# A two-layer hybrid mixer in fp32 on one core: TensorE in written order through the attention, two blocks turned ahead of their product, the next head's keys and values loaded one unit later

## The chip, the cores and the metric

The kernel runs on one core of one Trainium2 chip. The metric is the device time of one execution in microseconds (us). A run of the kernel before has a median of 3145.56 us.

## The reference

Two layers are computed for 1024 latent tokens and 256 context tokens, all in fp32, with a model width of 1024. In each layer one input projection feeds four token mixers: neighbourhood attention (`a`, 4 heads), multi-head latent attention (`m`, 4 heads), a recurrent scan (`lru`) and grouped-query attention (`g`, 4 heads). Their outputs are projected, weighted by sigmoid gates, summed, projected again and added to the stream. What matters here is the dense attention, which `g` and `m` share:

```python
def attend(q, keys, vals, scale):
    ...
    s = jnp.einsum('bkgqd,bknd->bkgqn', qg, keys, preferred_element_type=jnp.float32) * scale
    p = jax.nn.softmax(s, axis=-1).astype(vals.dtype)
    o = jnp.einsum('bkgqn,bknd->bkgqd', p, vals)
...
out = sum(jax.nn.sigmoid(ms[i]) * ((ys[i] * jax.nn.silu(zs[i])) @ w_branch[i]) for i in range(N_BRANCH)) @ w_out
```

Latent queries read all 1280 keys in `g` and `m`; in `a` they read a window of 8 by 16 latent tokens with a learned bias, and the context. Context queries read context only, and only in layer 0, because the second layer returns no context.

## The kernel before, in words

Every fp32 operand is held as a high and a low part, and a projection is three matmuls (high by high, low by high, high by low; `mm_b`, L284 to L286). ScalarE (ACT) casts the high part, VectorE (DVE) subtracts it from the source for the low part: `hi_lo` (L289 and L290) and, for weights, `split_w` (L238 and L239).

A layer runs through projections, the recurrent mixer woven between them, then the attention, then merge, and the output projection. In the attention twelve jobs, one for each head, follow each other: `g`, `m`, `a`, four heads each. A head goes through units of query tiles of 128 tokens: in layer 0 first a short unit of the two context tiles, in both layers then units of 3, 3 and 2 latent tiles. `attend` computes a unit:

- `scores` of one tile (L639): six matmuls for `g`, nine for `m`, into `wide`, three banks of PSUM of which there is one set. DVE moves it to `p` with its row minimum (L641), ACT takes the exponential (L615).
- `values` of a unit whose scores are done. It goes by blocks of 128 keys: `turn` transposes up to three tiles of `p` (L586) into one of two PSUM buffers `t`, ACT copies the high part to `ph` (L289), DVE subtracts for `pl` (L290); `product` adds the block into `pv` with two matmuls (L593 with `ph`, L594 with `pl`). The product of a block stands behind the turn of the next block. These steps are pumped between the scores of the following unit.
- `tick`, once per score tile and per block, adds now and then a group of six matmuls of the merge gates (`gates`, L284 to L286 into `g_att__mm`, `m_att__mm`, `a_att__mm`). Their weights come over ACT's DMA queue (L253), their results are copied by ACT (L938) and stored by a DMA that ACT issues (L939).

The queries of a unit come by DMAs on the queue of SyncE (SP) into one of three buffers `q` (L651, for `m` also L653 for the rotary part), one unit ahead. The keys `ks` (L660), values `vs` (L665) and for `a` two bias tables (`be`, `bm`) of the next head come on the same SP queue: `ahead_kv` is called at the first unit of a head.

The program is written in this order, but a list scheduler of the framework sets the order of every engine's queue, by priorities and a model of durations, unless an engine is pinned with `manual_schedule`. Tiles come from pools: `sl` holds 13 slots of 5 KB per partition (keys, values, probabilities, `y`, the scan's buffers), `wp` holds 10 pairs of high and low weights.

Of the kernel before, what the change touches and what calls it, by code (L numbers as in the profile page):

```python
# [17 lines left out]
KC = D // 128  # L18
# [21 lines left out]
UNITS = [(2, 3), (5, 3), (8, 2)]  # L40
NBIAS = (E_N + M_N) * 64
# [5 lines left out]
def hybrid_kernel(ctx: ExitStack, tc, a):  # L47
# [5 lines left out]
    wp = ctx.enter_context(tc.tile_pool(name="wp", bufs=10))  # L53
    sl = ctx.enter_context(tc.tile_pool(name="sl", bufs=13))
    tp = ctx.enter_context(tc.tile_pool(name="tp", bufs=2))
    sm = ctx.enter_context(tc.tile_pool(name="sm", bufs=6))
# [60 lines left out]
    def spare():  # L117

        turns[0] += 1
        tag = ("tmp", "ph", "tmp", "pl", "tmp", "ph", "pl")[turns[0] % 7]  # L120
        return tp.tile([128, 512], F32, tag=tag, name=nm("spare"), bufs=3 if tag == "tmp" else 2)
# [72 lines left out]
    def row_stats(src):  # L194
        st = sm.tile([128, 2, 6], F32, tag="bnst", name=nm("bnst"))
# [36 lines left out]
    def split_w(raw, shape):  # L232
        n = 1
        for d in shape[1:]:
            n *= d
        hi = wp.tile([128, 512], F32R, tag="whi", name=nm("whi"))
        lo = wp.tile([128, 512], F32R, tag="wlo", name=nm("wlo"))
# [7 lines left out]
    def load_w(src, shape):  # L245
# [8 lines left out]
        return split_w(raw, shape)  # L254

    def load_rows(w2, c0, n):
        return [load_w(w2[k * 128:(k + 1) * 128, c0:c0 + n], [128, n]) for k in range(KC)]
# [34 lines left out]
    def layer(l, xh, xl, need_ctx, gate, finish, side, side2, ahead=None):  # L292
# [27 lines left out]
        def put_t(dst, t, first, src, rows=128):  # L320
# [6 lines left out]
            hi = tp.tile([128, 4, 128], F32R, tag="ph", name=nm("th"), bufs=2)  # L327
# [8 lines left out]
        def put_v(dst, t, src3):  # L336

            n = src3.shape[1]
            vt = tp.tile([128, 4, 128], F32R, tag="ph", name=nm("vt"), bufs=2)
# [226 lines left out]
        def attend(h, unit, qs, y, rcp, scores, vt):  # L566
# [7 lines left out]
            queue.append([values(64 * (h % 2), y, qts, blocks, pts, vt), len(blocks) + 1])  # L574

        def values(o, y, qts, blocks, pts, vt):
# [5 lines left out]
            def turn(vb, q0, cols):  # L582
# [4 lines left out]
                ph = tp.tile([128, 512], F32R, tag="ph", name=nm("ph"), bufs=2)  # L587
# [8 lines left out]
            st = None  # L596
            for i, b in enumerate(blocks):
                nx = turn(*b)
                tick()
                if st:  # L600
                    product(i - 1, *st)
                st = nx
                yield
            product(nb - 1, *st)
# [111 lines left out]
        def m_steps():  # L716
            gm, mrope_c, mrope_s, wraws, wu = pre[0]
            wm = [split_w(r, [128, 416]) for r in wraws]
# [23 lines left out]
            def second(t, has_q, y, kr):  # L742
# [4 lines left out]
                ch = tp.tile([128, 512], F32R, tag="ph", name=nm("ch"), bufs=2)  # L747
# [138 lines left out]
        def attention(jobs):  # L886
# [22 lines left out]
            for n, (job, i) in enumerate(steps):  # L909
                label, h, branch, units, _, begin, _ = job  # L910
                fetch(n + 1)
                if i == 0:
                    j = jobs.index(job) + 1
                    if j < len(jobs):
                        ahead_kv(j)
                    head = begin(kv[label, h])
# [38 lines left out]
        for _ in att:  # L955
            pass
        flush()
# [58 lines left out]
        for c in range(KC):  # L1016
# [14 lines left out]
            wo[0].append(load_w(a["w_out"][l, c * 128:(c + 1) * 128, :512], [128, 512]))  # L1031
# [201 lines left out]
```

## Time and profile before

| | |
|---|---|
| three runs | 3131.25, 3145.56 (median), 3148.48 us |
| profiled execution: time / span | 3149.83 / 3148.0 us |
| granted TensorE clock, mean | 0.949 |
| attention of layer 0 | from 403 to 1163 us |
| attention of layer 1 | from 2085 to 2738 us |
| DMA, mean | 95 GB/s |

The profile is of one execution. Busy time of TensorE (PE) is the sum of stretches in which a matmul is shown at work. The clock of 1.00 is 2.4 GHz; where the rows show less, TensorE ran at 1.2 GHz in part of the stretch.

### The profile page before, as it was taken

The numbers are of one execution on the slowest core, as the hardware profiler recorded it, in microseconds if no ns is written. First come the engines' busy times: TensorE is split into PE (matmuls) and PEld (weight loads), VectorE is DVE, ScalarE is ACT, GpSimd is POOL, SyncE is SP. The second block draws the span as 40 slices with busy tenths as digits, with TensorE's granted clock in tenths as the row PEclk, the third lists the DMA queues.
The fourth block names the chain that finished last, engine by engine and source line by source line (L and its number), as shares of the span: only waits on it lengthen the run. The fifth ranks groups of instructions, "written<-read, shape, count | busy, mean of one in ns | idle before, by whom it ended". The sixth has DMA issues, their size and how long they took to land.

```text
span 3148.0 us, 39813 instructions
## 1 busy us (share of the span) xinstructions
PE 2837.8 (90%) x14458; PEld 2292.2 (73%) x14458; DVE 1554.1 (49%) x3147; ACT 1270.7 (40%) x2698; POOL 235.2 (7%) x327
## 2 busy tenths in 40 slices
PE   7987979998988999999789897998999897999878
PEld 3766868787877787776457685877887786788657
DVE  5653365554545551222368644366654464523366
ACT  4353364544444451111233435265544454512230
POOL 1210000000000000000342110000000000000141
PEclk9998989998999999999799999998999998999999
DMA  7232422222323222322462323322332233212252
GB/s 256 86 106 88 118 66 65 83 89 67 92 85 97 92 94 65 71 60 90 157 173 78 119 75 115 112 83 72 89 94 75 84 102 96 78 47 64 89 159 77
DMA packets 308782, 299.83 MB, mean 95 GB/s; under 512 B 24553, under 2 KB 245993, under 8 KB 308585
## 3 DMA queue, kind: packets, MB, share of 16 engines
q1 hardware_dynamic: 177384, 202.49, 21.3%
q10 hardware_dynamic: 131200, 94.79, 9.8%
q8 instruction: 114, 1.87, 0.3%
q14 instruction: 84, 0.68, 0.1%
HBM read 217.11 MB, written 80.10 MB: 94 GB/s over the span
## 4 chain that ended last, share of the span: by engine, by line
PE 65%; DMA 15%; DVE 7%; ACT 4%; POOL 3%; issue 3%; SPq 2%; ACTq 1%; POOLq 0%; DVEq 0%
PE wide L639 5%; PE merge__mm L284 4%; PE merge__mm L285 4%; PE merge__mm L286 4%; PE wide L284 2%; PE wide L285 2%; PE wide L286 2%; PE m_att__t L586 2%; PE a_att__mm L284 2%; PE a_att__mm L285 2%; PE a_att__mm L286 2%; DMA g_att__q<-start__qkg 2%; PE g_att__t L586 2%; PE m_att__mm L286 2%; PE m_att__mm L284 2%
## 5 line engine op out<-in xcount | busy, mean ns | idle before, releaser
L284 PE MATMUL merge__mm<-xh,merge__whi 128*128 128x512 f32 (+1 forms) x640 | 240.5, 376 | 1.2 <-DVE a_att__tmp L439 1.2
L285 PE MATMUL merge__mm<-xl,merge__whi 128*128 128x512 f32 (+1 forms) x640 | 236.7, 370 | 0.0
L286 PE MATMUL merge__mm<-xh,merge__wlo 128*128 128x512 f32 (+1 forms) x640 | 236.6, 370 | 0.0
L290 DVE TENSOR_TENSOR m_att__pl<-m_att__t,m_att__ph 128x384 fp32r<-128x384 f32 (+1 forms) x248 | 121.5, 507 | 141.3 <-ACT m_att__ph L289 138.2
L289 ACT CAST m_att__ph<-m_att__t 128x384 fp32r<-128x384 f32 (+1 forms) x248 | 105.7, 441 | 148.1 <-PE m_att__t L586 101.0
L238 ACT CAST merge__whi<-merge__wraw 128x512 fp32r<-128x512 f32 (+1 forms) x112 | 59.3, 530 | 236.0 <-PE merge__mm L285 179.3
L284 PEld LDWEIGHTS merge__mm<-xh,merge__whi 128*128 128x128 f32 x640 | 121.1, 189 | 41.5 <-issue 16.5
L239 DVE TENSOR_TENSOR merge__wlo<-merge__wraw,merge__whi 128x512 fp32r<-128x512 f32 (+1 forms) x112 | 64.5, 576 | 166.2 <-ACT merge__whi L238 158.4
L290 DVE TENSOR_TENSOR g_att__pl<-g_att__t,g_att__ph 128x384 fp32r<-128x384 f32 (+1 forms) x228 | 112.8, 514 | 68.0 <-ACT g_att__ph L289 64.6
L999 DVE TENSOR_TENSOR merge__tmp<-wide,merge__tmp 128x512 f32<-128x512 f32 (+1 forms) x80 | 50.9, 637 | 176.2 <-PE wide L286 168.3
L639 PE MATMUL wide<-g_att__ks,g_att__q 128*128 128x512 f32 (+1 forms) x400 | 112.4, 380 | 26.6 <-DMA g_att__q<-start__qkg 14.0
L286 PEld LDWEIGHTS merge__mm<-xh,merge__wlo 128*128 128x128 f32 x640 | 121.3, 189 | 20.7
L289 ACT CAST g_att__ph<-g_att__t 128x384 fp32r<-128x384 f32 (+1 forms) x228 | 99.6, 446 | 89.5 <-PE g_att__t L586 80.4
L285 PEld LDWEIGHTS merge__mm<-xl,merge__whi 128*128 128x128 f32 x640 | 121.2, 189 | 19.1
L284 PE MATMUL wide<-merge__uh,merge__whi 128*128 128x512 f32 (+1 forms) x240 | 100.5, 419 | 36.9 <-DVE merge__tmp L999 26.4
L284 PE MATMUL a_att__mm<-xh,a_att__whi 128*128 128x512 f32 (+1 forms) x320 | 126.2, 395 | 0.3 <-DVE a_att__tmp L439 0.3
L993 ACT ACTIVATE merge__tmp<-merge__mm 128x512 f32<-128x512 f32 (+1 forms) x80 | 44.2, 553 | 199.6 <-PE merge__mm L286 198.4
L593 PE MATMUL m_att__pv<-m_att__ph,m_att__vs 128*128 128x384 f32 (+1 forms) x228 | 88.8, 389 | 37.3 <-ACT m_att__ph L289 37.2
L285 PE MATMUL a_att__mm<-xl,a_att__whi 128*128 128x512 f32 (+1 forms) x320 | 121.9, 381 | 0.0
L641 DVE TENSOR_SCALAR_CACHE_REDUCE m_att__p<-wide 128x1280 f32<-128x1280 f32 (+1 forms) x72 | 98.7, 1371 | 46.1 <-PE wide L639 43.1
L286 PE MATMUL a_att__mm<-xh,a_att__wlo 128*128 128x512 f32 (+1 forms) x320 | 121.1, 380 | 0.0
L639 PE MATMUL wide<-m_att__ks,m_att__q 128*128 128x512 f32 (+1 forms) x400 | 120.8, 372 | 0.4 <-DVE m_att__p L641 0.4
(415 smaller groups left out, 8060.7 us busy)
## 6 DMA issues: line engine op xcount, KB each, us to landing
merge__wraw<-in_w_in_dram SPq DMA_DIRECT2D x64, 256.0 KB
mod__wm<-in_w_mod_dram SPq DMA_DIRECT2D x48, 256.0 KB
g_proj__wm<-in_w_mod_dram SPq DMA_DIRECT2D x16, 512.0 KB
a_att__wraw<-in_w_in_dram ACTq DMA_DIRECT2D x32, 256.0 KB
last__wraw<-in_w_out_dram SPq DMA_DIRECT2D x32, 256.0 KB
g_att__wraw<-in_w_in_dram ACTq DMA_DIRECT2D x28, 256.0 KB
m_att__wraw<-in_w_in_dram ACTq DMA_DIRECT2D x28, 256.0 KB
merge__wraw<-in_w_branch_dram SPq DMA_DIRECT2D x48, 128.0 KB
```

Source lines behind the costliest of these rows:

```text
L238: act.copy(hi[:, :n], raw[:, :n])
L239: dve.tensor_sub(lo[:, :n], raw[:, :n], hi[:, :n])
L284: pe.matmul(ps, wh, xh, start=first and k == 0, stop=False)
L285: pe.matmul(ps, wh, xl, start=False, stop=False)
L286: pe.matmul(ps, wl, xh, start=False, stop=last and k == nk - 1)
L289: act.copy(hi, src)
L290: dve.tensor_sub(lo, src, hi)
L586: pe.transpose(tb[:, i * 128:(i + 1) * 128], pts[q0 + i][:, col:col + 128], ident)
L593: pe.matmul(pv[:, qr], vt[:, vb, :], ph, start=i == 0, stop=False)
L639: pe.matmul(wide[:, c0:c0 + w], qs[:, j, qi * 128:(qi + 1) * 128], k[:, c0:c0 + w], start=j == 0, stop=j == len(ks) - 1)
L641: dve.tensor_scalar(pt[:, :nk], wide[:, :nk], -scale, None, ALU.mult, ALU.min, accum_out=nb)
L999: dve.tensor_mul(sgm[:, :g[1]], pb[:, :g[1]], sgm[:, :g[1]])
```

## The change

TensorE's queue keeps the order in which the program is written, from the first score of the attention to its last product. A block's product stands behind the turns of the two blocks that follow it (`AHEAD`), and the last products of a unit are steps of their own. The next head's keys and values are requested at a head's second unit. The slots become 16 and the weight pairs 6; to make room for eight weights at a time, half of the weights of a projection's eight row blocks (`far`) lie as a pair in one slot. A third `ph` buffer is added; some small tiles and a scratch area shrink. Line numbers move by 6 to 10.

```diff
+AHEAD = 2
-    wp = ctx.enter_context(tc.tile_pool(name="wp", bufs=10))
-    sl = ctx.enter_context(tc.tile_pool(name="sl", bufs=13))
+    wp = ctx.enter_context(tc.tile_pool(name="wp", bufs=6))
+    sl = ctx.enter_context(tc.tile_pool(name="sl", bufs=16))
-    sm = ctx.enter_context(tc.tile_pool(name="sm", bufs=6))
+    sm = ctx.enter_context(tc.tile_pool(name="sm", bufs=4))
...
-    def split_w(raw, shape):
+    def split_w(raw, shape, far=False):
...
+        if far:
+            both = slot(F32R, w=1024, s="wboth")
+            hi, lo = both[:, :512], both[:, 512:]
+        else:
+            hi = wp.tile([128, 512], F32R, tag="whi", name=nm("whi"))
+            lo = wp.tile([128, 512], F32R, tag="wlo", name=nm("wlo"))
...
-        return [load_w(w2[k * 128:(k + 1) * 128, c0:c0 + n], [128, n]) for k in range(KC)]
+        return [load_w(w2[k * 128:(k + 1) * 128, c0:c0 + n], [128, n], k >= 4) for k in range(KC)]
...
-            queue.append([values(64 * (h % 2), y, qts, blocks, pts, vt), len(blocks) + 1])
+            queue.append([values(64 * (h % 2), y, qts, blocks, pts, vt), len(blocks) + AHEAD])
...
-                ph = tp.tile([128, 512], F32R, tag="ph", name=nm("ph"), bufs=2)
+                ph = tp.tile([128, 512], F32R, tag="ph", name=nm("ph"), bufs=3)
...
-            st = None
+            turned = []
             for i, b in enumerate(blocks):
-                nx = turn(*b)
+                turned.append(turn(*b))
                 tick()
-                if st:
-                    product(i - 1, *st)
-                st = nx
+                if len(turned) > AHEAD:
+                    product(i - AHEAD, *turned.pop(0))
                 yield
-            product(nb - 1, *st)
+            for j, st in enumerate(turned):
+                product(nb - len(turned) + j, *st)
+                if j < len(turned) - 1:
+                    yield
...
                 if i == 0:
+                    head = begin(kv[label, h])
+                if i == 1:
                     j = jobs.index(job) + 1
                     if j < len(jobs):
                         ahead_kv(j)
-                    head = begin(kv[label, h])
...
-        for _ in att:
-            pass
-        flush()
+        with tc.manual_schedule(engines={mybir.EngineType.PE}):
+            for _ in att:
+                pass
+            flush()
...
-            wo[0].append(load_w(a["w_out"][l, c * 128:(c + 1) * 128, :512], [128, 512]))
+            wo[0].append(load_w(a["w_out"][l, c * 128:(c + 1) * 128, :512], [128, 512], 2 <= c < 6))
```

The first place is the SP queue in layer 0, inside the second `m` head, at the load of the third one's keys and values. Before:

```order
L653 DMA m_att__q_6511<-start__qkm_107 64x1x384
L651 DMA m_att__q_6674<-start__qkm_107 128x1x384
L660 DMA m_att__ks_6516<-start__qkm_107 128x1x1280
L665 DMA m_att__vs_6518<-start__vm_110 128x10x128
L653 DMA m_att__q_6674<-start__qkm_107 64x1x384
L651 DMA m_att__q_6674<-start__qkm_107 128x1x384
L653 DMA m_att__q_6674<-start__qkm_107 64x1x384
L651 DMA m_att__q_6755<-start__qkm_107 128x1x256
```

And now:

```order
L661 DMA m_att__q_6656<-start__qkm_107 64x1x384
L659 DMA m_att__q_6741<-start__qkm_107 128x1x256
L668 DMA m_att__ks_6661<-start__qkm_107 128x1x1280
L673 DMA m_att__vs_6663<-start__vm_110 128x10x128
L661 DMA m_att__q_6741<-start__qkm_107 64x1x256
L659 DMA m_att__q_6741<-start__qkm_107 128x1x256
L661 DMA m_att__q_6741<-start__qkm_107 64x1x256
L659 DMA m_att__q_6924<-start__qkm_107 128x1x256
```

The load stood among the queries of the head's third unit (three tiles, 384 columns) and stands among those of its fourth (two tiles, 256 columns).

The second place is TensorE's queue in the same head, behind its short unit: the end of the scores of one tile, what stands between, and the next tile's. Before:

```order
L639 MATMUL wide<-m_att__krs_5208,m_att__q_6511 128x256
L284 MATMUL m_att__mm_6627<-xh,m_att__whi_6623 128x256
L285 MATMUL m_att__mm_6627<-xl,m_att__whi_6623 128x256
L286 MATMUL m_att__mm_6627<-xh,m_att__wlo_6624 128x256
L284 MATMUL m_att__mm_6627<-xh,m_att__whi_6623 128x256
L285 MATMUL m_att__mm_6627<-xl,m_att__whi_6623 128x256
L286 MATMUL m_att__mm_6627<-xh,m_att__wlo_6624 128x256
L586 MATMUL m_att__t_6712<-ident,m_att__p_6520 128x128
L586 MATMUL m_att__t_6712<-ident,m_att__p_6583 128x128
L586 MATMUL m_att__t_6719<-ident,m_att__p_6520 128x128
L586 MATMUL m_att__t_6719<-ident,m_att__p_6583 128x128
```

And now:

```order
L647 MATMUL wide<-m_att__krs_5352,m_att__q_6497 128x256
L592 MATMUL m_att__t_6705<-ident,m_att__p_6502 128x128
L592 MATMUL m_att__t_6705<-ident,m_att__p_6563 128x128
L599 MATMUL m_att__pv_6678<-m_att__ph_6682,m_att__vs_6054 128x256
L600 MATMUL m_att__pv_6678<-m_att__pl_6683,m_att__vs_6054 128x256
L647 MATMUL wide<-m_att__ks_6052,m_att__q_6497 128x512 x2
L647 MATMUL wide<-m_att__krs_5352,m_att__q_6497 128x512
```

Ten matmuls and four more of the gates stood between the scores of the head's first two latent tiles; between those of the second and the third there are now four.

The third place is a block in the middle of a unit of the same head. Before, and then now:

```order
L586 MATMUL m_att__t_6828<-ident,m_att__p_6679 128x128
L586 MATMUL m_att__t_6828<-ident,m_att__p_6692 128x128
L586 MATMUL m_att__t_6828<-ident,m_att__p_6728 128x128
L593 MATMUL m_att__pv_6773<-m_att__ph_6803,m_att__vs_5796 128x384
L594 MATMUL m_att__pv_6773<-m_att__pl_6804,m_att__vs_5796 128x384
L586 MATMUL m_att__t_6838<-ident,m_att__p_6679 128x128
```

```order
L592 MATMUL m_att__t_6812<-ident,m_att__p_6665 128x128
L592 MATMUL m_att__t_6812<-ident,m_att__p_6692 128x128
L592 MATMUL m_att__t_6812<-ident,m_att__p_6714 128x128
L599 MATMUL m_att__pv_6759<-m_att__ph_6779,m_att__vs_6054 128x384
L600 MATMUL m_att__pv_6759<-m_att__pl_6780,m_att__vs_6054 128x384
L592 MATMUL m_att__t_6822<-ident,m_att__p_6665 128x128
```

The pair `ph_6803`, `pl_6804` belongs to the block turned before the one shown; `ph_6779`, `pl_6780` belongs to the one two blocks before.

## Rows read from the trace of the kernel before

**Rows 1.** The page, part 1 (busy time) and part 4 (the chain that ended last).

```profile
PE 2837.8 (90%) x14458; PEld 2292.2 (73%) x14458; DVE 1554.1 (49%) x3147; ACT 1270.7 (40%) x2698; POOL 235.2 (7%) x327
...
PE 65%; DMA 15%; DVE 7%; ACT 4%; POOL 3%; issue 3%; SPq 2%; ACTq 1%; POOLq 0%; DVEq 0%
```

**Rows 2.** TensorE by stretch, layer 0: length, busy (instructions), clock, DMA share, GB/s.

```profile
403.00:444.00 41.00, 22.69 (x91) 0.71 0.16 45
...
488.00:504.00 16.00, 12.04 (x60) 0.89 0.18 60
...
504.00:604.00 100.00, 99.70 (x596) 1.00 0.27 79
...
604.00:630.00 26.00, 20.03 (x100) 0.87 0.16 55
...
730.00:764.00 34.00, 23.54 (x121) 0.75 0.21 66
...
864.00:904.00 40.00, 29.91 (x164) 0.83 0.33 100
...
1004.00:1024.00 20.00, 11.48 (x55) 0.74 0.27 91
...
1064.00:1084.00 20.00, 14.92 (x67) 0.83 0.34 104
```

**Rows 3.** The same view in layer 1.

```profile
2106.00:2166.00 60.00, 47.14 (x248) 0.86 0.34 94
...
2386.00:2426.00 40.00, 35.00 (x182) 0.91 0.29 85
...
2426.00:2466.00 40.00, 36.03 (x185) 0.96 0.24 73
...
2466.00:2506.00 40.00, 34.15 (x178) 0.91 0.33 100
...
2600.00:2620.00 20.00, 15.86 (x77) 0.83 0.38 113
...
2646.00:2686.00 40.00, 28.30 (x138) 0.83 0.29 89
```

**Rows 4.** The timeline of SP's queue: start, duration, line, operation.

```profile
719.54 2.19 SPq L665 DMA_DIRECT2D m_att__vs<-start__vm  x1
721.77 15.28 SPq L653 DMA_DIRECT2D m_att__q<-start__qkm  x1
```

**Rows 5.** The timeline of ACT: start, duration, operation, idle before and releaser.

```profile
744.63 0.33 ACTq L939 DMA_DIRECT2D start__gates<-m_att__tmp  x1
745.28 0.37 ACT L289 CAST m_att__ph<-m_att__t 128x256 fp32r<-128x256 f32 x1 [10.09 <-DMA m_att__q<-start__qkm]
```

**Rows 6.** The timeline of TensorE, at the start of the attention and later.

```profile
417.12 0.39 PE L284 MATMUL g_att__mm<-xh,g_att__whi 128*128 128x512 f32 x1
...
417.34 0.39 PE L285 MATMUL g_att__mm<-xl,g_att__whi 128*128 128x512 f32 x1
...
438.12 2.50 PE L639 MATMUL wide<-g_att__ks,g_att__q 128*128 128x512 f32 x6 [8.59 <-DVE g_att__p L641]
...
745.71 0.58 PE L593 MATMUL m_att__pv<-m_att__ph,m_att__vs 128*128 128x256 f32 x1 [9.16 <-ACT m_att__ph L289]
```

**Rows 7.** The timeline of DVE at the start of layer 0's attention.

```profile
435.09 0.17 DVE L458 TENSOR_SCALAR lru__sp<-lru__lrucols 128x4 f32<-128x4 f32 x1 [12.88 <-DMA lru__lrucols<-in_lru_cols_dram]
```

**Rows 8.** The chain of waits, layer 1's start: start, duration.

```profile
2135.85 12.49 DMA g_att__wraw<-in_w_in_dram
```

**Rows 9.** Groups of instructions, both attentions: count, busy, mean ns, idle before and releasers.

```profile
L641 DVE TENSOR_SCALAR_CACHE_REDUCE m_att__p<-wide 128x1280 f32<-128x1280 f32 (+1 forms) x72 | 98.7, 1371 | 46.1 <-PE wide L639 43.1 <-PE m_att__t L586 2.1
...
L615 ACT ACTIVATE m_att__p<-m_att__p,m_att__nb 128x1280 f32<-128x1280 f32 (+1 forms) x72 | 91.6, 1272 | 42.1 <-DVE m_att__p L641 41.5
...
L289 ACT CAST m_att__ph<-m_att__t 128x384 fp32r<-128x384 f32 (+1 forms) x248 | 105.7, 441 | 148.1 <-PE m_att__t L586 101.0 <-DMA m_att__q<-start__qkm 26.4 <-DMA a_att__ks<-outp__qka 8.0
...
L290 DVE TENSOR_TENSOR m_att__pl<-m_att__t,m_att__ph 128x384 fp32r<-128x384 f32 (+1 forms) x248 | 121.5, 507 | 141.3 <-ACT m_att__ph L289 138.2
```

More of the change, by code (lines that the diff above doesn't have):

```diff
@@ L120, in spare @@
         tag = ("tmp", "ph", "tmp", "pl", "tmp", "ph", "pl")[turns[0] % 7]
-        return tp.tile([128, 512], F32, tag=tag, name=nm("spare"), bufs=3 if tag == "tmp" else 2)
+        return tp.tile([128, 512], F32, tag=tag, name=nm("spare"), bufs=2 if tag == "pl" else 3)
     def bank():
@@ L194, in row_stats @@
     def row_stats(src):
-        st = sm.tile([128, 2, 6], F32, tag="bnst", name=nm("bnst"))
+        st = sm.tile([128, 2, 6], F32, tag="bnst", name=nm("bnst"), bufs=2)
         for i in range(2):
@@ L235, in split_w @@
             n *= d
-        hi = wp.tile([128, 512], F32R, tag="whi", name=nm("whi"))
-        lo = wp.tile([128, 512], F32R, tag="wlo", name=nm("wlo"))
+        if far:
[4 more added lines that the diff above has]
+            lo = wp.tile([128, 512], F32R, tag="wlo", name=nm("wlo"))
         act.copy(hi[:, :n], raw[:, :n])
@@ L243, in split_w, with load_w @@
         return hi[:, :n], lo[:, :n]
-    def load_w(src, shape):
+    def load_w(src, shape, far=False):
         n = 1
@@ L253, in load_w @@
         wq[0].dma_start(dst, src)
-        return split_w(raw, shape)
+        return split_w(raw, shape, far)
     def load_rows(w2, c0, n):
-        return [load_w(w2[k * 128:(k + 1) * 128, c0:c0 + n], [128, n]) for k in range(KC)]
+        return [load_w(w2[k * 128:(k + 1) * 128, c0:c0 + n], [128, n], k >= 4) for k in range(KC)]
     def load_rows2(w2, c0):
@@ L326, in put_t @@
                 pe.transpose(pt[:r, i * 128:(i + 1) * 128], s, ident)
-            hi = tp.tile([128, 4, 128], F32R, tag="ph", name=nm("th"), bufs=2)
+            hi = tp.tile([128, 4, 128], F32R, tag="ph", name=nm("th"), bufs=3)
             lo = tp.tile([128, 4, 128], F32R, tag="pl", name=nm("tl"), bufs=2)
@@ L338, in put_v @@
             n = src3.shape[1]
-            vt = tp.tile([128, 4, 128], F32R, tag="ph", name=nm("vt"), bufs=2)
+            vt = tp.tile([128, 4, 128], F32R, tag="ph", name=nm("vt"), bufs=3)
             hi_lo(vt[:, :n, :64], vt[:, :n, 64:], src3)
@@ L717, in m_steps @@
             gm, mrope_c, mrope_s, wraws, wu = pre[0]
-            wm = [split_w(r, [128, 416]) for r in wraws]
+            wm = [split_w(r, [128, 416], k >= 4) for k, r in enumerate(wraws)]
             def first(t, ps):
@@ L746, in second @@
                     pe.transpose(pt[:, b * 128:(b + 1) * 128], y[:, b * 128:(b + 1) * 128], ident)
-                ch = tp.tile([128, 512], F32R, tag="ph", name=nm("ch"), bufs=2)
+                ch = tp.tile([128, 512], F32R, tag="ph", name=nm("ch"), bufs=3)
                 cl = tp.tile([128, 512], F32R, tag="pl", name=nm("cl"), bufs=2)
@@ L1221 @@
     }
-    nc = bacc.Bacc("TRN2", target_bir_lowering=False, num_devices=1, dynamic_dma_scratch_size=1024)
+    nc = bacc.Bacc("TRN2", target_bir_lowering=False, num_devices=1, dynamic_dma_scratch_size=64)
     arrays, args = {}, {}
```

## The prediction

> **What bounds the kernel now.** First the page: TensorE (PE) is busy 90% of the span and holds 65% of the chain that ended last; DMAs hold 15% of that chain, more than any other engine [rows 1]. So PE's work is the floor, and what can be won is PE standing still, or running at half its clock after it stood. Next the stretches of PE in the two attentions, which are the only stages whose order the change pins [rows 2, 3]. A clean stretch, as that from 504 to 604, is busy 99.70 of 100 us at a clock of 1.00. The losses sit in islands. I cost an island as its idle time plus (1 − clock) times its busy time, which is about what the clock takes away.
>
> - Layer 0 [rows 2]: the start, 403 to 444, loses 18.3 + 6.6 = 24.9 us. The six islands after it lose 5.3, 8.6, 16.3, 15.2, 11.5 and 7.6, together 64.5.
> - Layer 1 [rows 3]: the start, 2106 to 2166, loses 12.9 + 6.6 = 19.5 us. The five islands after it lose 8.2, 5.4, 8.9, 6.8 and 16.5, together 45.8.
>
> That is 155 us in all, and the most that better order can win here.
>
> Last, who makes an island. I follow the one at 730 to 764. PE waits 9.16 us at 745.71 for `ph`, ACT's copy [rows 6]. ACT waited 10.09 us, not for PE but for a DMA of `q`; in front of the copy it had issued a store of a gate [rows 5]. SP's queue shows why that `q` is late: the values `vs` of the next head go out at 719.54, and the next DMA, a piece of `q`, holds the queue for 15.28 us, to 737.05 [rows 4]. The load of keys and values stands in front of queries that are wanted soon, and ACT, which issues DMAs in between its copies, is held with them. Over both attentions ACT's `ph` in the `m` heads waits 26.4 us for such a `q` [rows 9]. The DMA engines themselves are busy only 0.13 to 0.34 of the time in these islands (0.16 to 0.38 with layer 1's) [rows 2, 3]: it is a queue that is full, not a bandwidth.
>
> **The change, part by part.**
>
> *The load one unit later, layer 0.* From 719.54 to the moment PE stopped (745.71 − 9.16 = 736.55) is 17 us of cover; ACT was released at 745.28 less its copy's hand-over, some 26 us after the load [rows 4 to 6]. Before, the cover was one short context unit and one unit of three tiles. Now it is two units of three tiles. Layer 0's attention takes 760 us for 144 score tiles (12 heads of 2 context and 10 latent tiles), 5.3 us each, so six tiles are an estimated 32 us. 32 is more than 26: where this pattern stands alone, the island goes. Two things keep part of it. ACT's DMAs stand earlier in line than PE's scores, so ACT meets the backlog before the 32 us are over; and for `a` heads the two bias tables follow in the same place. I keep 18 of the 64.5 us (three islands of the smaller size, 5.3 to 8.6): a gain of 46.5. The bounds are 0, if the backlog only meets other work, and 64.5.
>
> *The same in layer 1.* There is no context unit there: the cover was six latent tiles and is now five, the load stands before the next head's first queries and not before a head's last. PE's own need is no better covered; what changes is which of ACT's DMAs stand behind it. Between 0 and 45.8 I take two fifths, a gain of 18, because the islands here [rows 3] are the same kind at ACT but nothing in the order removes their cause.
>
> *Layer 1's start.* The chain shows a gate weight that lands 12.49 us after its issue [rows 8]; with 10 weight pairs five chunks of gate weights (two pairs each) could be ahead, now three can, and casts come later in ACT's queue. Between 0 and 19.5 I take a gain of 11.5.
>
> *Layer 0's start.* DVE stands 12.88 us for `lrucols` of the next layer's scan, hoisted in front of the scores [rows 7], and PE then waits 8.59 us at its scores [rows 6]. In the new order that instruction still stands there, ahead even of the second score. In the order before, 48 gate matmuls stood ahead of the first score and filled the scan's tail; matmuls of 512 columns start 0.22 us apart there (417.12, 417.34) [rows 6], so that filling was worth up to 11 us. Pinned, no gate matmul may pass the first score. I charge 8 us; bounds 0 and 11, plus a second wait of 8.59 if the scores stand twice.
>
> *Written order behind a short unit.* Scores use the one `wide`, and the next tile's wait for DVE's 1.371 us [rows 9]. Where 14 matmuls stood between two tiles there are now four, two transposes and two products, and behind the next unit's first scores its transposes need the last tile's exponential (1.371 + 1.272 us [rows 9]) sooner. By 0.22 us for a 512-column matmul, four smaller ones cover at most 0.5 us: 0.9 us are open at the first place, some 0.3 at the second. 12 heads by 1.2 us is 14 us, in layer 0 only. Bounds: 0 and 12 × 2.6 = 32.
>
> *Written order elsewhere.* Some 208 latent tiles (72 `g`, 72 `m`, 64 `a`, less what layer 0's short units already paid). A block turned needs ACT 0.441 and DVE 0.507 us [rows 9] before its product. One block behind, a transposition and a product stand between, about as much; two blocks behind, twice that, so that an exponential of 1.272 us in front of a copy is partly covered. The clean stretches carry the same load and idle 0.3% [rows 2]. I charge 5 us; bounds 0 and 62 (0.3 us for each tile).
>
> *Edits that I cost at nothing.* Slots, weight pairs, small tiles and the scratch: the counts of casts, subtractions and DMAs stay. In the projections and the woven scan `far` weights hold four slots, three of which are new. What hides a later weight is PE's backlog of other products; without that cover a slot that comes late costs one scan step. I bound it by −5 and +15 us.
>
> **The sum.** −46.5 − 18 − 11.5 + 8 + 14 + 5 = −49. The profiled execution took 3149.8 us, which makes 3100.8; it lies 4.3 above the median of the runs, 3145.56, so the forecast is **3097 us**.
>
> **The rivals.**
>
> *A. Nearly all of it goes.* If both layers' islands and layer 1's start go, and written order costs nothing: −64.5 − 45.8 − 19.5 = −130, that is 3016 us; with half of the costs charged, about 3030. For it: all islands have the queue in common. Against: layer 1's cover does not grow.
>
> *B. The backlog only moves.* The same bytes go through the same SP queue, and the piece behind them still waits 15 us [rows 4]; other queries and other stores of ACT are held instead. Then 3149.8 − 11.5 + 8 + 14 + 5 = 3165, less 4.3 = 3161 with the costs, 3134 without them. Against: of two loads of one kind only those with a short cover show an island, and 504 to 604 runs clean [rows 2]. The Trainium skill (Perfetto Trace Analysis, What "DMA-bound" means) holds that an issuing engine whose track is solid with DMA slices is bound by descriptor generation, and that larger descriptors are the cure; by that this move wins nothing. The trace agrees that the track is solid behind a load [rows 4], not that it is so between loads.
>
> *C. Slower: PE stands at every tile.* Before, the scheduler put gate matmuls where PE would wait; pinned, PE meets each score, transposition and product in program order, and a late DVE or ACT stops all that is behind it. Place: the wait of the next scores for `wide` and of transposes for PSUM's two `t`. Price: at 0.6 us for each of 208 tiles 125 us, against the other gains and losses of −46.5 − 18 − 11.5 + 8 = −68: 3149.8 + 57 − 4 = 3203 us. It decides from 68 / 208 = 0.33 us for each tile. For it: the first place above shows such a wait. Against: blocks are turned two ahead, and the gate matmuls still come every few steps. The Trainium skill (TensorE: Matmul & The Clock Gate, A second HAM failure mode: psum-queue depth-cycling) tells of a kernel whose frequent short pauses between groups of matmuls dropped the clock again and again; by the islands' ratio in layer 0 (45% on top of the idle time) that would make 3259. The trace so far speaks against it: from 2426 to 2466 PE idles 10% and the granted clock is 0.96 [rows 3].
>
> That the change does nothing, because the scheduler kept written order anyway, is ruled out by the rows of the order.
>
> **How the numbers follow.** A measurement of this kernel can tell a difference of about 0.5% (16 us) from none: below 3130 is faster, above 3161 slower. My forecast, 3065 to 3125: 0.50. Better than that, towards A: 0.13. B and half-way to it, 3125 to 3165: 0.20, of which 0.04 faster, 0.13 the same, 0.03 slower. C: 0.17, slower. Together 0.67, 0.13 and 0.20. The range from 3035 to 3160 holds the forecast, more than half of A's and nearly all of B's share, 0.8.
>
> **What would show it.** Right: layer 0's attention near 738 us (760 − 46.5 + 8 + 14 + 2.5) and layer 1's near 626 (653 − 18 − 11.5 + 2.5), no wait of `ph` for a `q` over 6 us in layer 0, short waits of under 1 us at `wide` behind each short unit, a mean clock above 0.95. B: the same number of islands at other heads, ACT still waiting for `q`. C: `wide` or `t` waiting for DVE some 200 times, and stretches that were clean idling 5% and more. The forecast is wrong if the start of layer 0 grows by over 20 us, if clean stretches get slower, or if projections and merge move by more than 15 us.

## The result and the profile after

The changed kernel is slower: 3329.15 us (median of 4 runs, 3327.03 to 3337.15) against 3140.98 for the kernel before; the ratio is 1.0606, with a 95% interval of 1.0568 to 1.0643. The forecast was 3097 us, in a range from 3035 to 3160. The profiled execution took 3329.8 us.

Busy time from the page of the changed kernel, to be held against [rows 1]:

```profile
PE 2875.8 (86%) x14458; PEld 2293.3 (69%) x14458; DVE 1567.8 (47%) x3147; ACT 1268.8 (38%) x2698; POOL 231.8 (7%) x327
```

TensorE (PE) has the same 14458 matmuls and 38 us more busy time; the span grew by 180, so most of the loss is idle time of TensorE.

TensorE by stretch, of the kernel before: the projections and scan of layer 0 (from the first product of `m_proj` to the first score), its attention (from the first score to the first product of the merge), its merge, the projections and scan of layer 1, its attention. The columns are length, busy, clock, DMA share, GB/s.

```profile
123.00:418.00 295.00, 256.44 (x1340) 0.94 0.32 96
418.00:1163.00 745.00, 681.26 (x3892) 0.95 0.27 83
1163.00:1565.00 402.00, 376.89 (x1753) 0.92 0.32 87
1824.00:2088.00 264.00, 232.47 (x1231) 0.94 0.32 98
2088.00:2731.00 643.00, 593.70 (x3213) 0.96 0.29 86
```

The same stretches of the changed kernel:

```profile
131.00:444.00 313.00, 258.71 (x1293) 0.88 0.30 89
444.00:1261.00 817.00, 704.35 (x3941) 0.96 0.24 75
1261.00:1649.00 388.00, 360.20 (x1751) 0.99 0.32 90
1908.00:2197.00 289.00, 243.13 (x1222) 0.88 0.30 89
2197.00:2920.00 723.00, 614.73 (x3246) 0.97 0.25 76
```

The attentions grew by 72 and 80 us. Ahead of them the projections grew by 18 and 25. The merge got 14 shorter. TensorE's granted clock in the attentions is no lower than before, 0.96 and 0.97; ahead of them it is 0.88, against 0.94.

TensorE's largest waits in the changed kernel (what it waited for; us in total, times, longest):

```profile
PE m_att__t L592 <- DVE m_att__pl L296: 44.0, 34, 7.9
PE wide L647 <- DVE g_att__p L649: 33.3, 11, 13.0
PE a_proj__mm L282 <- ACT a_proj__wboth L244: 32.9, 5, 16.8
PE g_att__t L592 <- DVE g_att__pl L296: 29.3, 31, 2.3
PE a_att__t L592 <- DVE a_att__pl L296: 29.1, 37, 2.6
...
PE wide L647 <- DVE m_att__p L649: 20.4, 8, 13.2
```

The islands of [rows 2, 3], where PE waited 4 to 10 us for `ph` behind a DMA, are mostly gone: waits of 3 us and more come to 37 us in layer 0's attention and 14 in layer 1's, 52 and 43 before. But the waits below 3 us went from 11 and 6 us to 79 and 96. Most of them stand at transposes, which wait for DVE's `pl` of two blocks before to free a PSUM buffer, and at scores, which wait for DVE to empty `wide`. The first layer's start still has its 13 us there, with DVE at the small table.

What one such wait is made of, in layer 1 (timeline; start, duration, engine, operation, idle before and its releaser):

```profile
2492.41 1.49 DVE L649 TENSOR_SCALAR_CACHE_REDUCE m_att__p<-wide 128x1280 f32<-128x1280 f32 x1 [0.65 <-PE wide L647]
...
2493.61 0.81 PE L592 MATMUL m_att__t<-ident,m_att__p 128*128 128x128 f32 x6
...
2493.95 1.36 ACT L623 ACTIVATE m_att__p<-m_att__p,m_att__nb 128x1280 f32<-128x1280 f32 x1 [2.77 <-DVE m_att__p L649]
...
2495.43 0.86 ACT L295 CAST m_att__ph<-m_att__t 128x384 fp32r<-128x384 f32 x2
...
2495.94 1.02 DVE L296 TENSOR_TENSOR m_att__pl<-m_att__t,m_att__ph 128x384 fp32r<-128x384 f32 x2 [2.02 <-ACT m_att__ph L295]
...
2496.55 0.78 PE L592 MATMUL m_att__t<-ident,m_att__p 128*128 128x128 f32 x3 [2.13 <-DVE m_att__pl L296]
```

DVE goes over the scores for 1.49 us. ACT takes the exponential behind it, 1.36 us, and only then copies the two blocks that PE had transposed at 2493.61. DVE subtracts; the first of the two PSUM buffers is free, and PE goes on after 2.13 us. The turns stood behind the scores in written order, and nothing else was allowed to pass them.

### The profile page after: what moved, and what is told of

It reads as the page before. It is cut to its first block, busy times and chain, and to the rows that moved or that the text cites. A ratio compares the mean times of both kernels' runs of the same rounds, so it can differ in the third digit from the quotient of the medians.

```text
span 3328.0 us, 40114 instructions
## 1 busy us (share of the span) xinstructions
PE 2875.8 (86%) x14458; PEld 2293.3 (69%) x14458; DVE 1567.8 (47%) x3147; ACT 1268.8 (38%) x2698; POOL 231.8 (7%) x327
## 3 DMA queue, kind: packets, MB, share of 16 engines
q1 hardware_dynamic: 177384, 202.49, 19.8%
## 5 line engine op out<-in xcount | busy, mean ns | idle before, releaser
L592 PE MATMUL m_att__t<-ident,m_att__p 128*128 128x128 f32 x616 | 108.6, 284 | 46.4 <-DVE m_att__pl L296 40.1
L592 PE MATMUL g_att__t<-ident,g_att__p 128*128 128x128 f32 x616 | 107.8, 284 | 31.4 <-DVE g_att__pl L296 29.3
L296 DVE TENSOR_TENSOR a_att__pl<-a_att__t,a_att__ph 128x384 fp32r<-128x384 f32 (+2 forms) x204 | 93.0, 463 | 79.3 <-PE a_att__pv L600 47.0
L647 PE MATMUL wide<-m_att__ks,m_att__q 128*128 128x512 f32 (+1 forms) x400 | 112.4, 363 | 20.4 <-DVE m_att__p L649 20.4
L647 PE MATMUL wide<-g_att__ks,g_att__q 128*128 128x512 f32 (+1 forms) x400 | 96.8, 379 | 38.3 <-DVE g_att__p L649 33.3
```

Of the source, the lines that this page charges most:

```text
L296: dve.tensor_sub(lo, src, hi)
L592: pe.transpose(tb[:, i * 128:(i + 1) * 128], pts[q0 + i][:, col:col + 128], ident)
L647: pe.matmul(wide[:, c0:c0 + w], qs[:, j, qi * 128:(qi + 1) * 128], k[:, c0:c0 + w], start=j == 0, stop=j == len(ks) - 1)
```

## The experiments

Each line is one kernel; the length of its stretches comes from its profile, in us, in the order of the rows above (projections 0, attention 0, merge 0, projections 1, attention 1). "Free" is a kernel whose TensorE order is left to the scheduler. "Old pools" is 13 slots, 10 weight pairs, no weights in slots; the smaller pool of small tiles and the smaller scratch area of the change stay in every kernel but "before" and e1.

| kernel | median us | stretches |
|---|---|---|
| before | 3140 to 3143 | 295, 745, 402, 264, 643 |
| changed: pinned, new pools, AHEAD 2 | 3329.2 | 313, 817, 388, 289, 723 |
| e1: before + later load | 3141.9 | 294, 741, 393, 261, 649 |
| e2: changed, free | 3141.9 | 314, 724, 388, 293, 612 |
| e3: changed, three `pl` | 3307.0 | 308, 803, 389, 284, 719 |
| e4: changed, old pools | 3308.7 | 291, 808, 403, 275, 732 |
| e5: free, old pools | 3123.3 | 291, 727, 394, 273, 636 |
| e6: e4, gates at scores | 3325.3 | 292, 808, 394, 271, 763 |
| e7: changed, AHEAD 1 | 3372.0 | 314, 824, 391, 290, 750 |
| e8: before + AHEAD 2 | 3119.8 | 289, 740, 405, 276, 621 |
| e9: e4, short exponential | 3260.4 | 293, 793, 407, 275, 700 |
| e10: e5, short exponential | 3140.5 | 292, 729, 401, 273, 641 |
| e11: e5, values in parts | 3169.8 | 292, 749, 385, 273, 667 |
| e12: e11, load at the first unit | 3203.9 | 288, 787, 391, 274, 657 |
| e13: e9, short row minimum | 3209.4 | 292, 786, 390, 273, 665 |
| e14: e8, small table early | 3149.5 | 293, 743, 401, 276, 635 |

The theory to start with: written order costs more than the later load gives. The rivals: the load's backlog only moves; the waits come from the two `pl` buffers; the pools are the cause.

**The parts, one at a time.** e1, the later load alone:

```diff
                 if i == 0:
+                    head = begin(kv[label, h])
+                if i == 1:
                     j = jobs.index(job) + 1
                     if j < len(jobs):
                         ahead_kv(j)
-                    head = begin(kv[label, h])
```

> The kernel before with one part of the change: the next head's keys and values requested at a head's second unit. Theory 1 (the move takes the islands away, the written order costs more than it gives): faster than before by 30 to 90 us, 3055 to 3115, with few waits of over 3 us for ph or q in the attentions. Rival (the backlog only moves, and the islands of the changed kernel went because TensorE is slower there and wants its queries later): within 15 us of before, as many islands of over 3 us as before, at other places.

Measured: 3141.9, ratio 0.9994 (0.9966 to 1.0022). The rival is right for the time and for the sum of the islands: TensorE's waits of 3 us and more in the attentions are 89 us, against 95. ACT's largest waits for DMAs of queries, keys, values and biases in this kernel:

```profile
ACT m_att__tmp L606 <- DMA a_att__ks<-start__qka: 16.4, 1, 16.4
...
ACT m_att__ph L289 <- DMA m_att__q<-outp__qkm: 12.8, 4, 3.8
...
ACT g_att__ph L289 <- DMA m_att__q<-start__qkm: 8.4, 1, 8.4
...
ACT g_att__ph L289 <- DMA m_att__q<-outp__qkm: 6.6, 1, 6.6
...
ACT m_att__ph L289 <- DMA a_att__vs<-outp__va: 6.4, 1, 6.4
...
ACT a_att__pa L619 <- DMA a_att__be<-in_na_bias_dram: 5.8, 1, 5.8
```

They come to 56 us. Before, the 26.4 and 8.0 us in [rows 9], one of 4.5 us for `m` and these three make 58:

```profile
ACT a_att__pa L619 <- DMA a_att__vs<-start__va: 7.7, 1, 7.7
...
ACT m_att__ph L289 <- DMA m_att__q<-outp__qkm: 6.6, 1, 6.6
...
ACT a_att__ph L289 <- DMA a_att__q<-outp__qka: 5.1, 1, 5.1
```

e2 takes the pinning away:

```diff
-        with tc.manual_schedule(engines={mybir.EngineType.PE}):
-            for _ in att:
-                pass
-            flush()
+        for _ in att:
+            pass
+        flush()
```

> The changed kernel without the pinning of TensorE's order; all else stays. Theory 1 (written order makes some 200 waits of 0.3 to 3 us, about 160 us over both attentions): 3329 falls by 110 to 200, to 3130 to 3220, and the short waits of transposes for DVE's pl and of scores for DVE's p vanish. Rival (the short waits come from AHEAD = 2 with two pl buffers, in whatever order): it stays above 3260, the waits for pl stay.

Measured: 3141.9, ratio 1.0008 (0.9985 to 1.0032). The 187 us are gone, and with them most of the short waits (31 us of waits between 0.3 and 3 us are left of 152; 14 before).

Its two attentions, 724 and 612 us, are 52 us shorter than before, and the projections ahead of them 48 longer. So something in the change does help the attentions, and something else spends it: the pools, which e4 undoes in the pinned kernel.

```diff
-    wp = ctx.enter_context(tc.tile_pool(name="wp", bufs=6))
-    sl = ctx.enter_context(tc.tile_pool(name="sl", bufs=16))
+    wp = ctx.enter_context(tc.tile_pool(name="wp", bufs=10))
+    sl = ctx.enter_context(tc.tile_pool(name="sl", bufs=13))
...
-        return [load_w(w2[k * 128:(k + 1) * 128, c0:c0 + n], [128, n], k >= 4) for k in range(KC)]
+        return [load_w(w2[k * 128:(k + 1) * 128, c0:c0 + n], [128, n]) for k in range(KC)]
...
```

> The changed kernel with 13 slots, 10 weight pairs and no weights in slots. Theory (far weights wait for slots that the woven scan holds; two waits of 16.8 and 12.6 us at a_proj and a longer scan, about 45 us before the attentions): the stretches before the two attentions get 35 to 60 us shorter, the attentions change by less than 20 us each: 3270 to 3295. Rival (the projections are late for another cause, such as the order of DMAs behind the earlier first queries): less than 15 us.

Measured: 3308.7, 20 us less; neither 3270 to 3295 nor the rival's number. The projections got 22 and 14 us shorter and the start of the kernel 9, together 45 as expected; layer 0's attention got 9 shorter (the wait of 13 us at its start is not there), its merge 15 longer and layer 1's attention 9 longer. Where the new pools stand, in the changed kernel's ACT timeline:

```profile
272.51 10.89 ACTq L339 DMA_DIRECT2D start__qkm<-m_proj__tl  x2
283.43 1.28 ACT L531 ACT_TABLE_LOAD   x1 [10.23 <-DVE m_proj__tl L296]
...
285.99 1.12 ACT L244 CAST a_proj__wboth<-a_proj__wraw 128x512 fp32r<-128x512 f32 x2
```

PE waited 16.8 us at `a_proj` for the cast at 285.99. ACT had been held 10.23 us by a store of `m_proj__tl` which it issues itself. The store is held with the old pools too, and PE then waits 10.4 us at `a_proj`'s transposes; so not all of the 16.8 is new. That the casts stand behind the store because their slots were still held was expected, and is not shown: the wait in the row shown is the store's.

e5 is e4 and e2 together, what is left being AHEAD = 2, the third `ph` and the later load.

> The changed kernel without the pinning and with 13 slots and 10 weight pairs: AHEAD = 2, a third ph buffer and the later load are what is left of the change. Theory: the run without pinning was as fast as before because attentions of 725 and 612 us (745 and 643 before) were paid back by stretches ahead of them that grew by 55 us with the new pools. With the old pools both hold: 3085 to 3110. Rival (the shorter attentions come from the 16 slots): the attentions return to 735 and 640, 3125 to 3145.

Measured: 3123.3, ratio 0.9945 (0.992 to 0.9971): faster than the kernel before, by less than expected (3085 to 3110). Its attentions:

```profile
412.00:1139.00 727.00, 673.98 (x3891) 0.96 0.27 85
2068.00:2704.00 636.00, 589.45 (x3213) 0.96 0.28 88
```

The projections are back to 291 and 273; the attentions came out 27 us longer than with 16 slots (e2), so the rival is right about that part. e8 leaves the later load out as well:

> The kernel before with AHEAD = 2 and a third ph buffer alone (not pinned, load at the first unit, 13 slots, 10 pairs). Theory (the third ph buffer and the later product let TensorE run on while ACT stands at a DMA): attentions 20 to 40 us shorter in sum, 3100 to 3125. Rival (only together with the later load, whose islands it makes short): 3135 to 3150.

Measured: 3119.8, ratio 0.9938 (0.9914 to 0.9962), the fastest kernel of the study and not to be told from e5 (its profile is of an execution of 3138.8 us, so its stretches say less). Both kernels with the later product and a third `ph` buffer are some 20 us faster than the one before; the later load gives nothing again. That the 20 us come from the product and the buffer is not shown: the smaller pool of small tiles and the scratch area are in both too, and e10 below shows that a free schedule, built anew for another edit, can move by 17 us. Nor was the later load tried alone with 16 slots; e2, which has both, has the fewest long waits of all free kernels, 48 us.

**What makes the pinned order slow.** e4 against e5, which differ in the pinning alone, is 3308.7 − 3123.3 = 185 us; their attentions differ by 1540 − 1363 = 177, that is 0.85 us for each of the prediction's 208 score tiles (192 latent ones and the 16 context tiles of `g` and `m`). e4's attentions, to be held against those of e5 above:

```profile
413.00:1221.00 808.00, 700.44 (x3939) 0.97 0.24 77
2159.00:2891.00 732.00, 622.39 (x3248) 0.96 0.25 77
```

TensorE idles 217 us in e4's and 100 in e5's: 118 of the 177 us are idle time. The other 59 are busy time: about a third of it is an estimated 18 us for 83 gate matmuls that stand outside these stretches in e5, at the 0.22 us of [rows 6]; the rest was not taken apart. e3 gives DVE a third `pl` and takes one slot away for it:

```diff
-                pl = tp.tile([128, 512], F32R, tag="pl", name=nm("pl"), bufs=2)
+                pl = tp.tile([128, 512], F32R, tag="pl", name=nm("pl"), bufs=3)
...
```

> The changed kernel with a third pl buffer (15 slots make room for it). Theory 2 (with two blocks turned ahead, two pl buffers let DVE write the next pl only behind the product that frees one, so that AHEAD = 2 hides nothing): the waits of transposes for pl, 102 us in the changed kernel, fall by more than half, the time by 50 to 120 us, to 3210 to 3280. Theory 1 in its plain form (the order itself, with two PSUM buffers t and one set of scores): the waits for pl stay within a third, the time falls by less than 30 us.

Measured: 3307.0, 22 us less. In its profile the projections are 10 us shorter and the attentions 18; a few us are lost elsewhere. The waits for `pl` did not fall, 112 us against 102:

```profile
PE m_att__t L592 <- DVE m_att__pl L296: 47.9, 38, 8.1
PE a_att__t L592 <- DVE a_att__pl L296: 33.2, 37, 3.4
PE g_att__t L592 <- DVE g_att__pl L296: 31.2, 34, 2.3
```

So two `pl` buffers are not the cause of these waits. e7 goes back to one block:

```diff
-AHEAD = 2
+AHEAD = 1
```

> The changed kernel with AHEAD = 1: pinned as before, each product one block behind its turn. Theory 3 (two PSUM buffers t limit the turns, AHEAD = 2 only moves the wait from the product to the third turn): 3315 to 3370, the waits for pl at transposes become waits of products for ph and pl of the same size. Rival (AHEAD = 2 hides a good part of the chain): over 3400.

Measured: 3372.0, 43 us more, 2 above the theory's range. The waits of transposes became waits of products, 98 us, about as long:

```profile
PE m_att__pv L599 <- ACT m_att__ph L295: 43.2, 43, 7.6
PE a_att__pv L599 <- ACT a_att__ph L295: 29.1, 35, 2.1
PE g_att__pv L599 <- ACT g_att__ph L295: 25.3, 33, 1.9
```

So the two blocks ahead do hide something, 43 us, and leave most of it. e6 puts all gate matmuls of a tile behind its scores, where DVE and ACT are busy with it:

```diff
-                tick()
+                tick(1.0 + len(blocks) / len(qts))
                 pump(len(qts) - qi)
...
                 turned.append(turn(*b))
-                tick()
```

> Pinned, old pools (3309 without this edit): all gate matmuls that a tile is due stand behind its scores, none among the blocks. Theory 3 (behind the scores stand DVE's 1.37 us and ACT's exponential of 1.27, and the copies of ph queue behind them, so the third turn waits for one of two PSUM buffers about 2 us; matmuls that need neither must stand just there): the waits of transposes for pl, 102 us, fall by more than half, the attentions by 50 to 120 us, 3190 to 3260. Rival (PE is bound by the pace of ACT and DVE at blocks, so that gate matmuls missing among the blocks make as many waits there): within 25 us of 3309.

Measured: 3325.3, 17 us more; the waits for `pl` rose from 102 to 163 us:

```profile
PE m_att__t L592 <- DVE m_att__pl L296: 68.0, 66, 7.6
PE g_att__t L592 <- DVE g_att__pl L296: 54.9, 59, 3.7
PE a_att__t L592 <- DVE a_att__pl L296: 40.4, 47, 2.2
```

The theory fell in this form, and the rival's number was met. In a stretch of `m` in layer 1 the waits were covered where twelve gate matmuls stood behind a tile's scores; where six stood, a wait of 1.5 us stayed, and among the blocks there was nothing left to cover anything. The scores' own waits for `p`, 54 us in e4, did go to 18.

Then the suspected passes themselves were cut. e9 takes the exponential of `g` and `m` over 128 columns in place of 1280 and leaves the others out; e10 does the same in the free kernel; e13 cuts DVE's pass over the scores as well.

```diff
-                act.activation(pt[:, c0:c1], pt[:, c0:c1], AF.Exp, bias=nb, scale=scale, accum_out=total)
+                act.activation(pt[:, c0:c0 + 128], pt[:, c0:c0 + 128], AF.Exp, scale=0.0, accum_out=total)
...
-                dve.tensor_scalar(pt[:, :nk], wide[:, :nk], -scale, None, ALU.mult, ALU.min, accum_out=nb)
+                pool.memset(pt[:, 128:nk], 1.0)
+                dve.tensor_scalar(pt[:, :128], wide[:, :128], -scale, None, ALU.mult, ALU.min, accum_out=nb)
```

> Pinned, old pools (3309), with the exponential of g and m cut from 1280 to 128 columns, 1.27 to about 0.3 us (it leaves out nine tenths of those exponentials and their bias). Theory 3 (ACT's exponential stands in front of the copies of ph, and pinned TensorE stands behind them): the waits of transposes for pl in g and m, 74 us, fall by more than two thirds, the attentions of g and m by 60 to 130 us, 3180 to 3250. Rival (DVE's 1.37 us for the scores, or the pace of two PSUM buffers, holds the turns): the waits fall by less than a third, 3270 or more.

> The same cut of the exponential without the pinning (3123 with the whole exponential). Theory 3: the scheduler had covered the exponential with other matmuls already, so it falls by less than 25 us, and the distance to the pinned kernel, 186 us, shrinks to less than 110. Rival (ACT's time bounds both): it falls by as much as the pinned one.

> As the pinned kernel with the short exponential (3260), and DVE's row minimum of g and m scores reads 128 columns in place of 1280 (1.37 to about 0.25 us; GpSimd fills the rest with ones; both outputs of the softmax are left out for nine tenths of the keys). Theory 3 in full (what stands in front of the copies is DVE's 1.37 and ACT's 1.27 us in a row behind the scores): the waits of transposes for pl in g and m, 47 us, and of scores for p, 42 us, fall to less than a third, 3150 to 3200. Rival (two PSUM buffers with a copy of 0.44 and a subtraction of 0.51 us hold the turns whatever else DVE and ACT do): the waits of transposes stay above 30 us, 3220 or more.

Measured: 3260.4 pinned (48 us less), 3140.5 free (17 more), 3209.4 pinned with both cuts (99 less). The waits for `pl` in `g` and `m`, whole, then with the short exponential, then with both cuts:

```profile
PE m_att__t L592 <- DVE m_att__pl L296: 43.4, 34, 8.0
PE g_att__t L592 <- DVE g_att__pl L296: 30.7, 32, 2.7
```

```profile
PE m_att__t L592 <- DVE m_att__pl L296: 28.1, 28, 6.8
PE g_att__t L592 <- DVE g_att__pl L296: 19.4, 24, 2.7
```

```profile
PE m_att__t L592 <- DVE m_att__pl L296: 35.1, 26, 11.5
PE g_att__t L592 <- DVE g_att__pl L296: 14.2, 21, 2.4
```

The last `m` row holds two waits of another kind, 11.5 and 7.4 us, with ACT at a DMA that it issues:

```profile
751.83 0.33 ACTq L949 DMA_DIRECT2D start__gates<-m_att__tmp  x1
752.20 0.37 ACT L295 CAST m_att__ph<-m_att__t 128x256 fp32r<-128x256 f32 x1 [11.85 <-DMA m_att__q<-start__qkm]
```

Without the longest of e4 (8.0) and of e9 (6.8) and these two, the waits go from 66 to 41 and to 30 us. That is between the two theories' numbers, and so are the times of e9 and e13. What the pair of e9 and e10 shows: the free kernel gains nothing from a shorter exponential, the pinned one gains 48, and the distance between them falls from 185 to 120 us (less than 110 was expected). That the free kernel's scheduler had covered the exponential with other matmuls fits this, but e10's schedule was built anew, and its 17 us more are not explained. With both passes cut the pinned kernel gets back 99 of the 185 us. So these passes of DVE and ACT are a large part of what pinning costs; whether they are over half would need the free kernel with both cuts, which was not run. The rest was not taken apart. A part of it is in the `a` heads, whose latent tiles neither cut touches (28.7 us of transposes, 12.4 us of scores in e13).

**Two tries at the islands.** e11 loads the values in five DMAs, one behind each score tile; e12 does so from a head's first unit on.

```diff
                 tick()
+                part()
                 pump(len(qts) - qi)
...
-            sp.dma_start(t.bitcast(F32), d[:, h, :].rearrange("(b p) e -> p b e", p=128))
+            for b in range(0, TT, 2):
+                parts.append((t.bitcast(F32)[:, b:b + 2, :],
+                              d[b * 128:(b + 2) * 128, h, :].rearrange("(b p) e -> p b e", p=128)))
```

> Not pinned, old pools, later load (3123), and the values of a head loaded in five DMAs of two key blocks each, one behind each score tile. Theory (one DMA of values holds SP's queue some 15 us, and ACT stands at its own DMAs with it): no SP issue of over 8 us behind values, waits of over 3 us in the attentions, 72 us in that kernel, fall by half, 3070 to 3100. Rival (the backlog moves again, since the bytes stay): 3110 to 3135.

> The same five parts with the load begun at a head's first unit (3120 with one DMA). Theory: 3070 to 3100, as with the later load, since the place no longer matters once no DMA holds the queue. Rival: as slow as with one DMA, 3110 to 3135.

Measured: 3169.8 and 3203.9, slower than both with one DMA; waits of 3 us and more in the attentions rose from 72 us (e5) to 124 and from 81 us (e8) to 154. Neither number was met. SP's queue in e11 shows that the edit did not do what it was meant to do:

```profile
725.40 8.01 SPq L666 DMA_DIRECT2D m_att__q<-start__qkm  x1
...
733.46 7.81 SPq L668 DMA_DIRECT2D m_att__q<-start__qkm  x1
...
741.36 4.75 SPq L559 DMA_DIRECT2D m_att__vs<-start__vm  x5
```

At this load the scheduler put the five parts together again, and the queue already stood 8.01 and 7.81 us at queries, with only the keys in front of them. So here the queue was full without the values' DMA. The test does not tell what spread parts would do.

e14 loads the scan's table of both layers at the start of the kernel, on top of e8.

```diff
-            cols = lc.tile([128, 22], F32, tag="lrucols", name=nm("lrucols"), bufs=1)
-            sp.dma_start(cols, a["lru_cols"][l])
+            if l == 0:
+                for j in range(2):
+                    lrucols.append(const.tile([128, 22], F32, name=nm(f"lrucols{j}")))
+                    sp.dma_start(lrucols[j], a["lru_cols"][j])
+            cols = lrucols[l]
```

> The kernel with AHEAD = 2 and a third ph buffer alone (3120), with the scan's small table of both layers loaded once at the start of the kernel, so that DVE does not stand for it in front of layer 0's scores. Theory: the wait of 8 to 13 us and the half clock behind it go, 3095 to 3112, faster than both kernels. Rival (PE waits for the first queries there anyway): 3113 to 3125.

Measured: 3149.5, ratio 1.0024 (0.9999 to 1.0048), slower than e8 by 30 us; neither number was met. (To make room it also gives four kinds of small tiles two buffers; what that costs was not tried by itself.) The wait of 8.3 us at the start went; one of 5.2 us for `ph` came 30 us later, and layer 1's attention got 14 us longer. The long waits of the attentions sum to 93 us, 81 in e8: taking one away did not make them fewer.

## Why the prediction was wrong

- **The largest term, written order elsewhere, failed.** It charged 5 us, with bounds of 0 and 62 (0.3 us for each of 208 tiles). Measured, e4 against e5: 177 us in the attentions, 0.85 us for each tile. The step that failed is the one that took the clean stretches of [rows 2] as a witness. They idle 0.3% in the scheduler's order, which pinning takes away. What that order had put in is seen in the clean stretch itself; this is `g_att__mm` alone, the gate matmuls, in the kernel before:

```profile
504.00:604.00 100.00, 57.12 (x251) 1.00 0.27 79
```

Of this stretch's 596 matmuls 251 are gate matmuls, and one of them is at work in 57 of the 100 us. That they stood just where DVE and ACT were late is read from the order and fits e2 and e5; e6, which put them all behind the scores by hand, did not get it back. The prediction then compared a block's 0.441 + 0.507 us with the cover of two blocks. It named ACT's exponential in front of the copies, but not DVE's pass in front of that, nor the two PSUM buffers of turned blocks, at which the third turn stops. The two passes take 1.49 + 1.36 us for a tile of 1280 keys; the means of 1.371 and 1.272 in [rows 9] have the short context tiles in them.
- **Three readings were wrong.** Layer 0 has 120 score tiles (12 heads of 2 context and 8 latent tiles) and not 144, so six of them are an estimated 38 us and not 32, which makes the cover look larger still. The 208 "latent" tiles are 192 and 16 context tiles. The DMA share in the islands is 0.16 to 0.34 in the rows; the 0.13 stands in none of them.
- **Rival C was the right case,** with its place (the scores' `wide`, the transposes' two `t`: 129 waits for DVE there, some 200 were named) and a price of 0.6 us for each tile that was too low; its point of decision was 0.33. It had been given a chance of 0.17. The rule that went with it in the Trainium skill (TensorE: Matmul & The Clock Gate, A second HAM failure mode: psum-queue depth-cycling), by which frequent short pauses would also cost the clock, is not borne out here: the changed kernel's attentions run at 0.96 and 0.97, with 139 waits between 0.3 and 3 us in them, 14 before.
- **The later load, −46.5 and −18: zero in a free kernel with 13 slots** (e1; e5 against e8). Rival B was right about the backlog, and the runs agree with what it took from the Trainium skill (Perfetto Trace Analysis, What "DMA-bound" means) in one thing: moving the load won nothing. That making descriptors is what holds the queue no run shows, and larger descriptors were not tried. The failed step is the cover of 32 us against 26: the queries now in time are one user of SP's queue, and ACT meets others. In the pinned kernel the islands did shrink, by 15 and 29 us. That a slower TensorE gives every DMA more time would explain it; this was only argued.
- **Edits costed at nothing, −5 to +15:** the new pools cost 45 us ahead of the attentions (e4: 9, 22 and 14) and give 15 back in layer 0's merge, and in the free kernel 27 in the attentions (e2 against e5): 20 net, pinned or free, outside the bounds. The cover that was named, a backlog of other products, was not there at `a_proj`, where PE stood 16.8 and 12.6 us (10.4 and 9.5 with the old pools).
- **The starts.** From 30 us before layer 0's first score to 40 us after it, TensorE idles 19.7 us before and 29.6 in the changed kernel, so the charge of 8 us was about the right size for the whole change. The order alone accounts for 7 of it with the new pools (22.6 in e2) and 2 with the old ones (22.0 in e4, 19.8 in e5). The wait of 13 us behind DVE goes with the new pools and not with the order: it is in e2 and not in e4. Layer 1's gain of 11.5 was of the right size in free kernels, but by luck: by the prediction's own way of costing, the stretch from 18 to 78 us behind the first score loses 19.5 us before, 9.0 in e1 and in e5, which have the later load and the old ten weight pairs, and 16.8 in e8, which has the earlier load. So it comes with the load, and not with the gate weights that the prediction named; other islands took the gain back. In the changed kernel that stretch loses 8.8 us, and short waits stand in front of it.
- **Behind a short unit, 14 us:** the waits at `wide` for DVE's `p` and `pa` are 64 us in all, 52 of them in layer 0, where two alone are 13 and 13. That leaves 25 us in layer 0 and 12 in layer 1, which has no short units; so the size may be right, but the places were not taken apart.

What helped had no term of its own in the sum: the kernel with AHEAD = 2 and a third `ph`, left to the scheduler, is some 20 us faster (e8, ratio 0.9938).

## What to carry to other kernels

A stretch that runs without a gap under a scheduler says what the scheduler fills in, not what the written order needs: before an engine is pinned, lay its new order against the whole latency of the engines it alternates with, the passes of the neighbouring step included, and count the buffers that limit how far it runs ahead. And moving the load that fills a queue need not mend the DMAs that are late on it: try the move alone, and look whether the waits turn up at other users of the queue.

## What the runs showed that was not expected

Moving the load, splitting it and taking one wait away each left the sum of long waits about where it was, or raised it: 89 us in e1 against 95 before, 72 in e5 against 81 in e8, 124 and 154 in e11 and e12, 93 in e14. The one free kernel in which they fell by half is e2, with 16 slots: 48 us. A free schedule is rebuilt by every edit: e5 and e8, which differ in one load, differ by 11 us in layer 0's merge (394 and 405), which the edit does not touch. With a tenth of the exponentials, the free kernel was no faster (3140.5 against 3123.3).
